# A routed-expert kernel: row gathers without empty slots, one-hot products for one pair instead of two, one more weight place, larger combination pieces, another order in the last pair

## The chip, the cores and the metric

The kernel runs on one core of a Trainium2 chip. The metric is the device time of one execution in microseconds (us). The program before was run three times: 1092.27, 1098.74 and 1100.58 us, median 1098.74. A core has five engines that work side by side: TensorE (PE; its weight loads are shown as PEld), VectorE (DVE), ScalarE (ACT), GpSimd (POOL) and SyncE (SP). They synchronise by semaphores. Sixteen DMA engines move data for all of them; each issuing engine has its own queue. Data live in SBUF (128 partitions) and in PSUM, the small memory that TensorE writes.

## What is computed

One backbone block on 512 latent tokens of width 1024 with 256 context tokens: neighbourhood attention beside a recurrent branch, merged and projected, then a mixture of experts with 32 experts, of which each token uses two, then a final RMSNorm. All is float32. The part that the change touches is the mixture:

```
def hier_moe(h, wg, bg, we, be, w1, w3, w2):
    p_top, g_idx = lax.top_k(softmax(h32 @ wg + bg), 1)      # 1 of 4 groups
    ev, e_idx = lax.top_k(le_sel, TOP_K)                     # 2 of its 8 experts
    gate = p_top * softmax(ev)
    eid = g_idx * EXPERTS_PER_GROUP + e_idx
    ...
        return (silu(xblk @ w1[e]) * (xblk @ w3[e])) @ w2[e]     # 1024 -> 512 -> 1024
    ...
    out = zeros.at[buf_tok].add(yb * buf_w[:, None])
x = x + ga2 * hier_moe(ada_rmsnorm(x, g_ffn, sh2, sc2), ...)
return rms(x) * g_final
```

## The kernel before, in words

The first part (to about 560 us) computes the modulation, the two branches and their merge. In it SP loads the weights of the up-projection (`wlo<-in_ua`, `wlo<-in_ul`, L56) and of the output projection (`woraw`, L680) in an order in which loads of expert weights (`w<-in_ew`, L908) are interleaved by hand. From about 560 to 617 us the output projection runs for 4 token tiles of 128 tokens (`outp`, matmuls L762 to L764), and behind each tile the router: logits, choice of experts, rank of the token among those of its expert (`route`). Each expert has 64 slots; two experts make a pair, and the 128 slots of a pair are the 128 rows of one gather. There are 16 pairs.

The slot table. For each token tile the kernel writes, per chosen expert, a record (token number, gate, 1/rms) into a zeroed table in DRAM, `std`, with an indirect scatter from POOL (L815, eight in all). ACT loads the eight partial tables (L885), VectorE adds them up (`stok`, L886) and casts the token numbers to integers (`toki`, L888). An empty slot holds token 0 with gate 0. `rows` (L933) is an indirect DMA from POOL that gathers, for one pair, 128 rows of the normalised stream `nd` (4 KB each) by `toki`. `turn` (L939 to L946) scales those rows by the 1/rms on ACT, transposes them on TensorE in two halves and applies the modulation while it copies them from PSUM (`xg`, the transposed input of a pair).

Pairs 0 and 1 don't wait for the table. For them `onehot0` builds a one-hot matrix (128 tokens x 256 slots) from the router's registers (L821, L822), and `gather0` (L828) multiplies the normalised tokens with it. That needs the tokens split into two parts of reduced precision, `yh` and `yl` (L803, L804). `scatter` (L961, L963) later turns the same one-hot matrices into the matrices that send results back (`ot`), and into the gates.

The mixture's loop runs over pairs `pr` and steps `k` of 128 input channels: `gu(pr, k)` (L1082) is 8 matmuls against one weight piece of 1 MB (gate and up parts of two experts). After gu(pr, 7) come silu (L976), the product `hm` (L977), its transposes (L981) and the copy `hT` (L984). Then gu(pr+1, 0), and `down(pr, v)` (L1094), two halves v of the output width with two pieces of 1 MB each. So a pair uses 12 pieces, and 192 are loaded in all. `combine` multiplies the result by the gated modulation `ga` (L992), splits it (L993, L994) and sends it back to the token tiles: for each half four pieces of two matmuls (L999, L1000), each added to `x` by VectorE (L1002). `step(c, 2)` runs two such pieces between two gu steps.

What sets the order. A scheduler keeps each engine's instructions in the order of the code, unless `queued` and `tc.issue_after` pin one behind another. Weight pieces rotate through WR + WL + 3 = 23 places of SBUF (9 on the right side, 11 on the left, 3 lent early); piece n+23 is issued by SP when the matmuls on piece n are over. Two of the first places (EARLY) are given to other buffers after their first use. `late` says which of the first loads come last in SP's order.

The last pair: the accumulators of the second half are seeded with x by matmuls with the identity (L1039), `finish` adds the last results to them (L1058), squares and sums (L1061), and scales out of PSUM (L1049, L1050). The four output tiles go out by L1051.

Of the kernel before, what the change touches and what calls it, by code (L numbers as in the profile page):

```python
# [19 lines left out]
D = 1024  # L20
# [11 lines left out]
WR, WL = 9, 11  # L32
# [5 lines left out]
def tile_block(ctx: ExitStack, tc: tile.TileContext, A, out):  # L38
# [670 lines left out]

    sg = xp.tile([128, 4, 6], F32, name="sg")  # L710
# [3 lines left out]
    for q in range(2):  # L714
        V.tensor_copy(rec[:, :, q, 0], pidx[:, 0:4])
# [13 lines left out]
    ohp = R.enter_context(pool("oh", "right"))  # L729
    oh = [ohp.tile([128, 256], F32R, name="oh", bufs=4) for _ in range(4)]  # L730
# [14 lines left out]
    l2.enter_context(pool("gap")).tile([128, 10 * 256], F32, name="gap")  # L745
    with pool("p3") as p3, ExitStack() as xtx:
# [5 lines left out]
        n2h, n2l = [], []  # L752
        def outp(nh, i):
# [107 lines left out]
        pg0 = [ps3.tile([128, 256], F32, name=z, bufs=b) for z, b in (  # L861
# [10 lines left out]
        pg0.append(ps3.tile([128, 256], F32, name="pr"))  # L872
# [5 lines left out]
    with ExitStack() as wx:  # L878
        left = [wx.enter_context(pool(f"w{i}")) for i in range(WR, WR + WL)]
        wpool += [left[4], left[10], *left[5:10], *left[0:4]]  # L880
# [5 lines left out]
        V.reduce_sum(stok.rearrange("p n k -> p (n k)"), s8[:, 0:384].rearrange("p (i x) -> p x i", i=8), axis=AX.X)  # L886
# [220 lines left out]
        for pr in range(NE // 2):  # L1107
            for k in range(1 if pr else 0, NK):
# [10 lines left out]
                if cmb and k == 1:  # L1119
                    step(cmb[0], 2)  # L1120
# [305 lines left out]
```

## Time and profile before

| | us |
|---|---|
| runs | 1092.27, 1098.74, 1100.58 (median 1098.74) |
| the profiled execution | 1095.06 |
| its span | 1093.0 |
| TensorE busy | 1019.6 (93%), granted clock 0.977 of full |
| VectorE busy | 574.7 (53%) |
| ScalarE busy | 437.3 (40%) |
| GpSimd busy | 98.4 (9%) |
| moved by DMA | 303.60 MB, mean 278 GB/s |

The span is the time between the first and last instruction in the trace. Instruction rows give start and duration, engine, line of the kernel, what is written from what, and how many; a bracket gives the idle time ahead of it and what ended it. SPq, ACTq and POOLq rows are DMA issues; their duration is that of the issue, with the time to the last issue where several stand in one row. PEclk is the clock that TensorE was granted, as a share of full speed.

### The profile page before, as it was taken

The numbers are of one execution on the slowest core, as the hardware profiler recorded it, in microseconds if no ns is written. First come the engines' busy times: TensorE is split into PE (matmuls) and PEld (weight loads), VectorE is DVE, ScalarE is ACT, GpSimd is POOL, SyncE is SP. The second block draws the span as 40 slices with busy tenths as digits, with TensorE's granted clock in tenths as the row PEclk, the third lists the DMA queues.
The fourth block names the chain that finished last, engine by engine and source line by source line (L and its number), as shares of the span: only waits on it lengthen the run. The fifth ranks groups of instructions, "written<-read, shape, count | busy, mean of one in ns | idle before, by whom it ended". The sixth has DMA issues, their size and how long they took to land. (4 is left out here: it accounts for less than half of the span.)

```text
span 1093.0 us, 13843 instructions
## 1 busy us (share of the span) xinstructions
PE 1019.6 (93%) x5148; PEld 619.8 (57%) x5148; DVE 574.7 (53%) x1172; ACT 437.3 (40%) x775; POOL 98.4 (9%) x167
## 2 busy tenths in 40 slices
PE   8998999799898989869999889999999999999995
PEld 7787768567776877657888534333333333333332
DVE  5679669567856966576547623333333353322324
ACT  4335783577387458813222222222222222222214
POOL 0012011101201120110000200000000000000001
PEclk9999999899999989989999989999999999999998
DMA  9487246425633552285694899999999999999993
GB/s 373 179 246 223 92 148 198 116 83 162 189 92 111 202 135 73 74 308 168 205 371 177 315 417 418 421 421 421 420 420 420 421 420 422 420 420 420 420 421 148
DMA packets 62857, 303.60 MB, mean 278 GB/s; under 512 B 10282, under 2 KB 10562, under 8 KB 37188
## 3 DMA queue, kind: packets, MB, share of 16 engines
q1 hardware_dynamic: 44212, 254.54, 58.7%
q0 software_dynamic: 12512, 40.93, 12.1%
q10 hardware_dynamic: 6064, 7.22, 1.9%
q8 instruction: 41, 0.67, 0.2%
q14 instruction: 28, 0.23, 0.1%
HBM read 286.72 MB, written 9.65 MB: 271 GB/s over the span
## 5 line engine op out<-in xcount | busy, mean ns | idle before, releaser
L1082 PE MATMUL g<-w,xg 128*64 128x512 f32 x1024 | 240.5, 605 | 2.6 <-DMA w<-in_ew 2.4
L1082 PEld LDWEIGHTS g<-w,xg 128*64 128x64 f32 x1024 | 66.2, 137 | 129.9 <-issue 114.6
L48 PE MATMUL pj<-hh,whi 128*128 128x512 f32 x320 | 132.1, 413 | 2.4 <-ACT gi L498 1.9
L49 PE MATMUL pj<-hl,whi 128*128 128x512 f32 x320 | 128.2, 400 | 0.0
L50 PE MATMUL pj<-hh,wlo 128*128 128x512 f32 x320 | 127.9, 400 | 0.0
L1094 PE MATMUL y<-w,hT 128*64 128x512 f32 x512 | 114.1, 594 | 4.8 <-DMA w<-in_ew 4.8
L1002 DVE TENSOR_TENSOR x<-x,pc 128x512 f32<-128x512 f32 x121 | 77.8, 684 | 70.5 <-PE pc L1000 70.5
L946 ACT ACTIVATE xg<-pg,sh2col,s2col 128x128 f32<-128x128 f32 x112 | 42.1, 457 | 131.5 <-PE pg L943 131.5
L60 DVE TENSOR_TENSOR wlo<-wlo,whi 128x1024 fp32r<-128x1024 f32 (+1 forms) x60 | 68.9, 1148 | 46.8 <-ACT whi L59 46.7
L59 ACT CAST whi<-wlo 128x1024 fp32r<-128x1024 f32 (+1 forms) x60 | 59.4, 990 | 82.1 <-DMA wlo<-in_wcol 44.3
L993 ACT CAST y_h<-hm 128x512 fp32r<-128x512 f32 x31 | 19.2, 619 | 161.0 <-PE pc L999 93.7
L1094 PEld LDWEIGHTS y<-w,hT 128*64 128x64 f32 x512 | 35.1, 137 | 81.9 <-issue 60.1
L992 DVE TENSOR_TENSOR hm<-y,ga 128x512 f32<-128x512 f32 x31 | 21.4, 692 | 110.6 <-PE y L1094 102.2
L48 PEld LDWEIGHTS pj<-hh,whi 128*128 128x128 f32 x320 | 61.4, 192 | 19.9 <-ACT gi L498 3.5
L50 PEld LDWEIGHTS pj<-hh,wlo 128*128 128x128 f32 x320 | 61.1, 191 | 15.1
L49 PEld LDWEIGHTS pj<-hl,whi 128*128 128x128 f32 x320 | 61.5, 192 | 12.4
L977 DVE SCALAR_TENSOR_TENSOR hm<-hm,stok,g 128x512 f32<-128x512 f32 x14 | 10.5, 748 | 95.2 <-PE g L1082 95.2
L999 PE MATMUL pc<-y_h,ot 128*128 128x512 f32 x121 | 54.4, 449 | 1.2 <-ACT y_h L993 1.2
L999 PEld LDWEIGHTS pc<-y_h,ot 128*128 128x128 f32 x121 | 22.8, 188 | 53.3 <-issue 48.7
L1000 PE MATMUL pc<-y_l,ot 128*128 128x512 f32 x121 | 48.5, 400 | 0.1
L496 PE MATMUL pj<-xc,ga 128*128 128x256 f32 (+1 forms) x128 | 47.7, 500 | 0.0
L933 POOL DMA_INDIRECT xr<-nd,toki x14 | 13.2, 944 | 367.0 <-PE pt L981 287.7
(393 smaller groups left out, 1753.9 us busy)
## 6 DMA issues: line engine op xcount, KB each, us to landing
w<-in_ew SPq DMA_DIRECT2D x191, 1024.0 KB
wlo<-in_wcol SPq DMA_DIRECT2D x40, 512.0 KB
m<-in_wm POOLq DMA_DIRECT2D x32, 512.0 KB, 3.9
wm<-in_wm SPq DMA_DIRECT2D x8, 1024.0 KB
bias<-in_rpb POOLq DMA_DIRECT2D x32, 128.0 KB, 2.4
kr<-khl POOLq DMA_DIRECT2D x16, 256.0 KB, 6.4
gd<-ga ACTq DMA_DIRECT2D x16, 256.0 KB
wlo<-in_ul SPq DMA_DIRECT2D x8, 512.0 KB
```

Of the source, the lines that this page charges most:

```text
L48: PE.matmul(o, wh, hh, start=start, stop=False)
L49: PE.matmul(o, wh, hl, start=False, stop=False)
L50: return PE.matmul(o, wl, hh, start=False, stop=stop)
L59: S.copy(hi[:, :n], raw[:, :n])
L60: V.tensor_tensor(lo[:, :n], raw[:, :n], hi[:, :n].bitcast(F32), op=ALU.subtract)
L496: m = PE.matmul(pg[:, 0:n], lw[:, 128 * w:128 * w + 128], xc[:, s0:s0 + n], start=True, stop=True)
L946: S.activation(xg[:, k, :], pg[:, k % 4, :], AF.Identity, bias=sh2col[:, k:k + 1], scale=s2col[:, k:k + 1])
L999: PE.matmul(pc, ot[:, i, :], y_h, start=True, stop=False)
L1000: m = PE.matmul(pc, ot[:, i, :], y_l, start=False, stop=True)
L1002: V.tensor_add(x2[:, i, ns], x2[:, i, ns], pc)
L1082: m = PE.matmul(pgu[pr][v][64 * e:64 * e + 64, :], xg[pr][:, k, 64 * e:64 * e + 64], w[:, v, e, :], start=(k == 0), stop=(k == NK - 1))
L1094: m = PE.matmul(py[64 * e:64 * e + 64, :], hT[:, k, 64 * e:64 * e + 64], w[:, k % 2, e, :], start=(k == 0), stop=(k == 3))
```

## The change

Nine edits. (1) WL is 12 instead of 11: one more place of 1 MB, and SP's order begins with three expert pieces where it began with two. `late` moves by three with it, and the places are handed out in another order. (2) The one-hot matrices have 128 columns (pair 0 only) and carry 1/rms as their value, so that `gather0` multiplies `x2` itself in one matmul where there were two, and `yh` and `yl` are gone. (3) The table's token numbers are stored plus one; after the sum one is subtracted, and an empty slot becomes a number past the last token. (4) The gather has a bound, past which a row is left out; its target is one tile `xr`, zeroed once. (5) Pairs 1 to 15 are gathered, pair 1 in the place where pair 2's gather was issued. (6) All pairs take gate and return matrix from the table. (7) `combine` runs four pieces at once, after gu(pr+1, 0) with down(pr), and after gu(pr+1, 3), where it ran two pieces at four places; transposes, pieces and broadcasts share four PSUM banks. (8) In the last pair three seeds run after gu(15, 4), and the first half's pieces lie inside the second half's down. (9) Some small operations of the final norm are taken out of its loop.

```
-WR, WL = 9, 11
+WR, WL = 9, 12
...
-        V.tensor_copy(rec[:, :, q, 0], pidx[:, 0:4])
+        V.tensor_scalar(rec[:, :, q, 0], pidx[:, 0:4], 1.0, None, op0=ALU.add)
...
-                S.activation(n2h[i][:, hs], x2[:, i, hs], AF.Copy, scale=st[:, 4:5])
-                V.scalar_tensor_tensor(n2l[i][:, hs], x2[:, i, hs], st[:, 4:5], n2h[i][:, hs].bitcast(F32),
-                                       op0=ALU.mult, op1=ALU.subtract)
...
-            V.tensor_scalar(t, iot[:, 0:256], sgt[i][:, 0:1], None, op0=ALU.is_equal)
-            V.scalar_tensor_tensor(oh[i], iot[:, 0:256], sgt[i][:, 1:2], t, op0=ALU.is_equal, op1=ALU.add)
+            V.tensor_scalar(oh[i], iot[:, 0:128], sgt[i][:, 0:1], r, op0=ALU.is_equal, op1=ALU.mult)
+            V.tensor_scalar(t, iot[:, 0:128], sgt[i][:, 1:2], r, op0=ALU.is_equal, op1=ALU.mult)
+            V.tensor_tensor(oh[i], oh[i], t, op=ALU.add)
...
-                for h in (n2h, n2l):
-                    PE.matmul(pg0[k], h[i][:, 128 * k:128 * k + 128], oh[i],
-                              start=(i == 0 and h is n2h), stop=(i == 3 and h is n2l))
+                PE.matmul(pg0[k], x2[:, i, 128 * k:128 * k + 128], oh[i], start=(i == 0), stop=(i == 3))
...
-        toki = p4.tile([128, NE // 2], I32, name="toki")
-        V.tensor_copy(toki, stok[:, :, 0])
...
+        V.tensor_scalar(stok[:, :, 0], stok[:, :, 0], 1.0, None, op0=ALU.subtract)
+        V.tensor_scalar(tokx, stok[:, :, 0], 0.0, 2.0 * T, op0=ALU.is_lt, op1=ALU.mult)
+        V.tensor_tensor(toki, tokx, stok[:, :, 0], op=ALU.add)
+        xr = p4.tile([128, D], F32, name="xr")
+        G.memset(xr, 0.0)
...
-        late = (*range(WR + 5, WR + 9), EARLY[1], *range(WR + 9, WR + WL + 3))
+        late = (*range(WR + 8, WR + 12), EARLY[1], *range(WR + 12, WR + WL + 3))
...
-            G.indirect_dma_start(xr, None, nd[:, :], bass.IndirectOffsetOnAxis(ap=tok, axis=0))
+            G.indirect_dma_start(xr, None, nd[:, :], bass.IndirectOffsetOnAxis(ap=tok, axis=0), bounds_check=T - 1,
+                                 oob_is_err=False)
...
-        cmb, xr = [], rows(toki[:, 2:3])
+        rows(toki[:, 1:2])
+        cmb = []
...
-                if cmb and k == 1:
-                    step(cmb[0], 2)
                 if cmb and k == 3:
-                    step(cmb[1], 2)
+                    step(cmb[1], 4)
...
-                if 0 < pr < LAST and k == 5:
-                    xg[pr + 1] = p4.tile([128, NK, 128], F32, name="xg", bufs=2)
-                    turn(xr, xg[pr + 1], 0, stok[:, pr + 1, 2:3])
-            if cmb:
-                step(cmb[1], 2)
+                if pr < LAST and k == 5:
+                    xg[pr + 1] = halves()
+                    turn(xg[pr + 1], 0, stok[:, pr + 1, 2:3])
+                if pr == LAST and k == 4:
...
+                    for i in range(3):
+                        with queued():
+                            m = seed(i)
...
-            if pr > 1:
-                ot = places(stok[:, pr, 0:1])
+            ot = places(stok[:, pr, 0:1])
...
-                step(cmb[0], 2)
+                step(cmb[0], 4)
...
+            py = down(pr, 1, range(0, 3))
+            for i in range(3):
+                norm_half(next(part))
+            py = down(pr, 1, range(3, 4), py)
             norm_half(next(part))
-            with tc.issue_after(m):
-                py = down(pr, 1)
```

Three places show what stands where. First TensorE in the first pair, before (L1082 is gu, L961 and L963 turn the one-hot matrices, L981 transposes hm, L1094 is down):

```order
L1082 MATMUL g_5657<-w,xg 64x512 x2
L1082 MATMUL g_5658<-w,xg 64x512 x2
L961 MATMUL pt<-ident,oh 128x128 x4
L963 MATMUL pg<-sg,oh 128x6 x4
L1082 MATMUL g_5657<-w,xg 64x512 x2
L1082 MATMUL g_5658<-w,xg 64x512 x2
L981 MATMUL pt<-ident,hm 128x128 x4
L1082 MATMUL g_5733<-w,xg 64x512 x2
L1082 MATMUL g_5734<-w,xg 64x512 x2
L1094 MATMUL y_5739<-w,hT 64x512 x8
```

The same place of the change (L1079 is gu, L945 transposes gathered rows `xr`, L1032 spreads the modulation `ga`):

```order
L1079 MATMUL g_5604<-w,xg_5540 64x512 x2
L1079 MATMUL g_5605<-w,xg_5540 64x512 x2
L945 MATMUL pc<-ident,xr 128x128 x4
L1079 MATMUL g_5604<-w,xg_5540 64x512 x2
L1079 MATMUL g_5605<-w,xg_5540 64x512 x2
L1079 MATMUL g_5604<-w,xg_5540 64x512 x2
L1079 MATMUL g_5605<-w,xg_5540 64x512 x2
L1032 MATMUL pc<-ga_5654,ones 128x512 x2
L945 MATMUL pc<-ident,xr 128x128 x4
L981 MATMUL pc<-ident,hm 128x128 x4
L1079 MATMUL g_5690<-w,xg_5630 64x512 x2
L1079 MATMUL g_5691<-w,xg_5630 64x512 x2
```

The two gu steps ahead of hm's transposes, 6 and 7, now stand behind transposes of gathered rows, the first half of pair 1's.

Second ACT at the same time, before (L885 loads the table, L976 is silu, L939 scales gathered rows):

```order
L885 DMA s_5575<-std_85 128x48
L885 DMA s_5575<-std_86 128x48
L966 CAST ot<-pt 128x512
L976 ACT_TABLE_LOAD
L976 ACTIVATE hm<-g_5657 128x512
L984 COPY hT<-pt 128x512
L1034 COPY ga_5695<-pc 128x512 x2
L993 CAST y_h<-hm 128x512
L939 ACTIVATE xr<-xr,stok 128x1024
```

And now (L878 loads the table, L941 scales, L948 copies the transposed rows):

```order
L878 DMA s_5523<-std_85 128x48
L878 DMA s_5523<-std_86 128x48
L941 ACTIVATE xr<-xr,stok 128x1024
L948 ACTIVATE xg_5630<-pc,sh2col,s2col 128x128 x4
L976 ACT_TABLE_LOAD
L976 ACTIVATE hm<-g_5604 128x512
L1033 COPY ga_5654<-pc 128x512 x2
L948 ACTIVATE xg_5631<-pc,sh2col,s2col 128x128 x4
L984 COPY hT<-pt 128x512
```

The scaling of the gathered rows moved from behind the first pair's silu, copies and cast to directly behind the table's loads.

Third TensorE at the end, before (L1039 seeds, L1094 down, L999 and L1000 the pieces, L1058 the last products):

```order
L1039 MATMUL g_8048<-x_4626,ident 128x512
L1094 MATMUL y_8051<-w,hT 64x512 x8
L1094 MATMUL y_8076<-w,hT 64x512 x8
L999 MATMUL pc<-y_h,ot 128x512
L999 MATMUL pt<-y_h,ot 128x512
L999 MATMUL y_8121<-y_h,ot 128x512
L1000 MATMUL pc<-y_l,ot 128x512
L1000 MATMUL pt<-y_l,ot 128x512
L1000 MATMUL y_8121<-y_l,ot 128x512
L1058 MATMUL pg<-hm,ot 128x512
```

And now (L1038 seeds, L1092 down, L998 and L999 the pieces, L1057 the last products):

```order
L1038 MATMUL g_8017<-x_4626,ident 128x512
L1092 MATMUL y_8019<-w,hT 64x512 x8
L1092 MATMUL y_8033<-w,hT 64x512 x6
L998 MATMUL pc<-y_h,ot 128x512
L999 MATMUL pc<-y_l,ot 128x512
L998 MATMUL g_8032<-y_h,ot 128x512
L999 MATMUL g_8032<-y_l,ot 128x512
L998 MATMUL y_8019<-y_h,ot 128x512
L999 MATMUL y_8019<-y_l,ot 128x512
L1092 MATMUL y_8033<-w,hT 64x512 x2
L998 MATMUL pc<-y_h,ot 128x512
L999 MATMUL pc<-y_l,ot 128x512
```

One seed stands ahead of down(15) where four stood, and three of the pieces moved from behind it to ahead of its last two weight blocks.

## Rows read from the trace of the kernel before

**Rows 1.** Windows: PE, PEld, DVE, ACT, POOL busy (instructions), clock, DMA share, GB/s.
```profile
600.00:620.00 20.00, 15.25 (x136) 12.63 (x136) 18.41 (x114) 7.65 (x21) 7.44 (x8) 1.00 0.74 282
615.00:620.00 5.00, 4.92 (x35) 3.35 (x35) 3.62 (x15) 2.90 (x8) 2.46 (x3) 1.00 0.21 41
620.00:630.00 10.00, 10.00 (x48) 3.16 (x44) 0.00 (x0) 0.00 (x0) 0.00 (x0) 1.00 1.01 411
930.00:1050.00 120.00, 113.45 (x500) 40.87 (x500) 35.32 (x56) 26.64 (x54) 2.82 (x3) 1.00 1.01 421
1070.00:1080.00 10.00, 10.00 (x42) 4.11 (x39) 4.39 (x9) 2.36 (x7) 0.93 (x1) 1.00 0.08 33
```
**Rows 2.** Waits of SP's queue in 930 to 1093: total, times, longest.
```profile
SPq L908 <- DMA w<-in_ew: 99.5, 46, 2.7
```
**Rows 3.** Timeline of ACT: silu of pairs 2 and 10, start and duration.
```profile
696.43 0.60 ACT L976 ACTIVATE hm<-g 128x512 f32<-128x512 f32 x1 [1.23 <-PE g L1082]
...
915.38 0.60 ACT L976 ACTIVATE hm<-g 128x512 f32<-128x512 f32 x1 [1.23 <-PE g L1082]
```
**Rows 4.** Timeline of SP: issues of expert weights before 621.
```profile
476.30 0.80 SPq L908 DMA_DIRECT2D w<-in_ew  x2
...
534.61 13.61 SPq L908 DMA_DIRECT2D w<-in_ew  x8
...
564.63 38.00 SPq L908 DMA_DIRECT2D w<-in_ew  x9
...
617.69 3.12 SPq L908 DMA_DIRECT2D w<-in_ew  x5
```
**Rows 5.** Timeline of TensorE from 617, and the window 637 to 640.
```profile
617.85 12.24 PE L1082 MATMUL g<-w,xg 128*64 128x512 f32 x56
...
636.03 0.66 PE L981 MATMUL pt<-ident,hm 128*128 128x128 f32 x4 [2.69 <-DVE hm L977]
636.61 3.53 PE L1082 MATMUL g<-w,xg 128*64 128x512 f32 x8
...
637.00:640.00 3.00, 3.00 (x10) 0.81 (x8) 0.44 (x1) 0.30 (x1) 0.00 (x0) 0.50 1.01 409
```
**Rows 6.** Timeline: the slot table's way on ACT's queue, DVE, POOL and ACT.
```profile
623.53 9.13 ACTq L885 DMA_DIRECT2D s<-std  x3
...
639.56 0.80 DVE L886 TENSOR_REDUCE stok<-s 128x48 f32<-128x384 f32 x1 [3.60 <-DMA s<-std]
640.40 0.17 DVE L888 CAST toki<-stok 128x16 int32<-128x16 f32 x1
...
641.56 1.00 POOL L933 DMA_INDIRECT xr<-nd,toki  x1 [22.74 <-issue]
...
651.25 1.15 ACT L939 ACTIVATE xr<-xr,stok 128x1024 f32<-128x1024 f32 x1 [1.09 <-DMA xr<-nd,toki]
```
**Rows 7.** Groups of VectorE in 595 to 617: busy, mean ns.
```profile
L822 DVE SCALAR_TENSOR_TENSOR oh<-iot,sg,oht 128x256 fp32r<-128x256 f32 x4 | 1.9, 481 | 0.0
```
**Rows 8.** DMA issues: KB each, median us to landing; the gathers' own spread.
```profile
bias<-in_rpb POOLq DMA_DIRECT2D x32, 128.0 KB, 2.4
...
std<-rec,si POOLq DMA_INDIRECT x8, 6.2
...
DMA to landing us min/median/max: 8.4/9.7/9.9
```
**Rows 9.** Timeline of TensorE behind the early expert pieces.
```profile
489.57 0.50 PE L48 MATMUL pj<-oh,whi 128*128 128x512 f32 x1 [2.83 <-ACT whi L59]
```
**Rows 10.** Timeline of TensorE in the last pair.
```profile
1062.40 1.94 PE L1082 MATMUL g<-w,xg 128*64 128x512 f32 x8 [0.55 <-DMA w<-in_ew]
...
1069.29 7.09 PE L1094 MATMUL y<-w,hT 128*64 128x512 f32 x32
1076.30 0.50 PE L999 MATMUL pc<-y_h,ot 128*128 128x512 f32 x1
...
1077.80 1.02 PE L1058 MATMUL pg<-hm,ot 128*128 128x512 f32 x2
```

More of the change, by code (lines that the diff above doesn't have):

```diff
@@ L751, in tile_block @@
         lgs = p3.tile([128, 4, 36], F32, name="lgs")
-        n2h, n2l = [], []
+        oh = [p3.tile([128, 128], F32, name=f"oh{i}") for i in range(4)]
         def outp(nh, i):
@@ L955, in scatter @@
         def scatter(oh, x):
-            pt = ps4.tile([128, 4, 128], F32, name="pt")
-            pq = ps4.tile([128, 256], F32, name="pg")
-            with queued():
-                for i in range(4):
-                    PE.transpose(pt[:, i, :], oh[i].bitcast(F32), ident)
-                for i in range(4):
-                    m = PE.matmul(pq[:, 0:6], oh[i].bitcast(F32), sg[:, i, :], start=(i == 0), stop=(i == 3))
-            tail[0] = tail[0] and m.ins
+            pt = ps4.tile([128, 4, 128], F32, name="pc", bufs=4)
+            pq = ps4.tile([128, 256], F32, name="pc", bufs=4)
+            for i in range(4):
+                PE.transpose(pt[:, i, :], oh[i].bitcast(F32), ident)
+            for i in range(4):
+                PE.matmul(pq[:, 0:6], oh[i].bitcast(F32), sg[:, i, :], start=(i == 0), stop=(i == 3))
             ot = p5.tile([128, 4, 128], F32R, name="ot", bufs=2)
@@ L983, in act, with combine @@
             hT = p5.tile([128, 4, 128], F32, name="hT")
-            return hT, S.copy(hT, pt).ins
-        def combine(v, py, ot, last=False):
+            return hT, S.copy(hT, pt).ins, pt
+        def combine(v, py, ot, banks=None):
             ns = slice(512 * v, 512 * v + 512)
@@ L995, in combine @@
             for i in range(4):
-                pc = ps4.tile([128, 512], F32, name=("y0" if i == 2 else "pt")) if last and i else ps4.tile(
-                    [128, 512], F32, name="pc", bufs=2)
+                pc = banks[i] if banks else ps4.tile([128, 512], F32, name="pc", bufs=4)
                 with queued():
@@ L1038, in seed, with finish @@
         def seed(i):
[L1039 to L1041 removed]
+            return PE.matmul(acc[i], ident, x2[:, i, 512:1024], start=True, stop=False)
+        def finish(py, ot):
             ns = slice(512, 1024)
@@ L1081, in gu, with down @@
                     for e in range(2):
-                        m = PE.matmul(pgu[pr][v][64 * e:64 * e + 64, :], xg[pr][:, k, 64 * e:64 * e + 64],
+                        m = PE.matmul(pgu[pr][v][64 * e:64 * e + 64, :], xg[pr][k // 4][:, k % 4, 64 * e:64 * e + 64],
                                       w[:, v, e, :], start=(k == 0), stop=(k == NK - 1))
             tail[0] = m.ins
-        def down(pr, v):
-            py = ps4.tile([128, 512], F32, name=f"y{v}")
-            for k in range(4):
+        def down(pr, v, ks=range(4), py=None):
+            py = py or ps4.tile([128, 512], F32, name=f"y{v}")
+            for k in ks:
                 if k % 2 == 0:
-                    w = weights(pr, 8 + 2 * v + k // 2)
+                    dw[0] = weights(pr, 8 + 2 * v + k // 2)
+                w = dw[0]
                 with queued():
@@ L1213, in tile_block @@
                 for v in range(2):
-                    PE.matmul(pgu[v], xg[:, k, 0:128], w[:, v, :], start=(k == 0), stop=(k == NK - 1))
-            hT, after = act(pgu, gate)
+                    PE.matmul(pgu[v], xg[k // 4][:, k % 4, :], w[:, v, :], start=(k == 0), stop=(k == NK - 1))
+            hT, _, _ = act(pgu, gate)
             for v in range(2):
```

107 lines of the change are left out of this document (46 added, 61 removed).

## The prediction

> **What bounds the kernel now.** I read the windows first. From 620 on the DMA engines are full: 411 GB/s at a share of 1.01 over 620–630, 421 GB/s over 930–1050, and almost nothing after 1071 (1070–1080: share 0.08, that is 0.8 us of transfers) [rows 1]. What they move are the experts' weights, 192 pieces of 1.0486 MB, 12 for each of the 16 pairs of experts. At 421 GB/s a piece takes 1.0486 / 0.421 = 2.49 us. Second, the waits of SP at the end: in 930–1093 its weight loads wait 99.5 us for earlier loads, and for almost nothing else [rows 2]. TensorE is the nearer limit earlier: its silu starts of pair 2 and pair 10 lie 218.95 us apart, 27.37 a pair [rows 3], while 12 pieces and one gather take 31.1. So the stream sets the end, and the kernel ends a fixed tail after its last piece. A change is worth what it does to (a) the moment from which the stream never stops, and what has landed then, (b) the bytes after it, (c) the tail.
>
> For (a): SP had issued 2 pieces at 476, 8 from 534.61, and nine from 564.63 to 602.63, 19 in all, when the next five went out at 617.69 [rows 4]. In between the DMA engines ran dry: share 0.21 in 615–620 [rows 1]. So 19 pieces lay in SBUF at about 619.8, two microseconds behind that issue.
>
> Last, the start of the MoE on TensorE: gu(0,·), 8 steps of 8 matmuls, runs from 617.85 to 633.34 with only the one-hot transposes between; after 2.69 us of waiting the granted clock is 0.50 in 637–640, that is the lower level, 1.2 GHz, and a step takes 3.53 instead of some 1.75 us (12.24 / 7) [rows 5]. The pair's last step ends at 633.34, where that wait begins. Beside it, and hidden, runs the round trip of the slot table: its last three loads wait on ACT's queue until 632.66 (they reuse semaphores of weight pieces still in flight), VectorE gets the table at 639.56, POOL issues the gather at 641.56, and ACT scales its rows at 651.25 [rows 6]. Nobody waits for that: these rows are pair 2's, and pairs 0 and 1 came out of the one-hot products.
>
> **The change, part by part.** *One-hot products for pair 0 only.* Pair 1 is now gathered, and TensorE's order puts the transposes of its rows between gu(0,5) and gu(0,6). So the hidden round trip becomes a wait of TensorE. It starts near 617.85 + 6 x 1.75 = 628, or 2 to 3 us sooner, as VectorE loses the yl products and half of each one-hot matrix; the sum doesn't hang on the start. It ends so:
> - The seventh and eighth table loads now wait for pieces 26 and 27. Piece 15 waits on an out-projection matmul near 599.7, so data flow from 601.7 (the same two microseconds), with 14 landed. Before, 600–620 carried 282 GB/s x 20 us = 5.6 MB, of which I put 0.8 (an estimate) to other transfers than pieces 15 to 19. Full, at 421 GB/s, 601.7–619.8 carries 7.6; less 0.8 that is 6.5 pieces, so 20.5 have landed at 619.8 (1.5 more than before). At 411 GB/s (2.55 a piece) piece 27 lands at 636.4 and piece 29 at 641.5.
> - The last load: 6.9 us before (632.66 to 639.56) with the stream full behind it. Lower bound 2.4, the median landing of the bias loads [rows 8]. Only two pieces are queued with it now; I take 5.5: 642.2.
> - VectorE: 0.80, three small steps like toki's 0.17, and two places products, which I set at 0.48 each from the old one-hot row [rows 6, 7]: 2.3, giving 644.5; POOL's issue one more, 645.5.
> - The gather: 9.7 us to landing as before, with 128 rows beside a full stream; lower bound 6.2, the small scatters [rows 8]. 69 rows beside an idle stream: I take 7.5. Then ACT's 1.15: 654.2.
>
> TensorE thus stands for 26 to 29 us. After that it runs four transposes (0.6), gu(0,6) at the low clock (3.5) and gu(0,7) (2 to 2.7), to 661; then silu and hm, and gu(1,0) ends near 665.5.
>
> Does the stream suffer? There are now 24 places: pieces 25 to 29 go into those that gu(0,0) to gu(0,5) free (two of these were lent out and are gone), 30 needs gu(0,7) and 31 needs gu(1,0). So after piece 29 at 641.5 the DMA engines stand, but for 30, until 665.5 + 2 = 667.5; 30 pieces have landed then and 162 remain. **This is the main term.**
>
> *Row gathers leave out empty slots.* Counted from the inputs' routing, 1,024 of the 2,048 slots are filled, 71 in pair 0, 69 in pair 1, so pairs 2 to 15 gather 884 rows of 4 KB, 3.62 MB or 8.6 us of stream. Before, 14 gathers moved all 128 slots: 14 x 1.25 = 17.4 us.
>
> Sum for the stream: 667.5 + 162 x 2.49 (403.4) + 8.6 = 1079.5. The same sum for before, 619.8 + 173 x 2.49 (430.8) + 17.4 = 1068.0, is 3 short of 1071 (table loads, broadcast rows, a slower start); half of that still lies ahead at 667.5. So the last piece lands at 1081, **10 later**.
>
> *One more weight place* lets a third piece go at 476.7. It stands in front of the up-projection weights that SP issues next, whose cast TensorE already awaited 2.83 us before 489.57 [rows 9]. A piece is 2.49 us; delay 0 to 2.5, I take **+1**, since the load's wait on an earlier piece may absorb part.
>
> *Larger combination pieces.* Two switches between gu and pieces fewer a pair. Even if that saves nothing, TensorE at 27.37 a pair ends gu(15,7) at 661 + 15 x 27.37 = 1072; the stream, 10 later than before, lets it end at 1074 (before: 1064.34 [rows 10]). So it is worth 0, hidden behind the stream, with 2 us to spare and whatever it does save. On the other side, four PSUM banks now serve transposes and pieces, and a fifth piece has to wait until VectorE has added an earlier one. I bound that by 1 us a pair, about two wide VectorE operations like the 0.48-us one [rows 7]; then it shows.
>
> *Last pair.* Down(15) began at 1069.28, 4.9 us after gu(15,7), behind four seeds; its weights were there at 1071, so it could have been up to 2.8 earlier before its last piece held it [rows 1, 10]. Three seeds now run at k = 4. The three combination pieces between its end and the final matmuls (1076.30 to 1077.80) move inside it and cost the same there. Between 0 and -2.8; I take **-2**, since the last results still pass one after the other through squares and scaling.
>
> Sum: 1095.06 (the profiled run: span 1093.0 and 2.1 around it) + 10 + 1 - 2 = **1104**. That run lies 3.7 under the median of those shown, 1098.74; against it 1104 is +0.5%. A change of about 1% (11 us) is what a measurement of this kernel can tell.
>
> **The rivals.** *A short stall* (0.20). By the lower bounds, load 2.4 and gather 6.2, TensorE resumes 4.4 earlier: 1100. The Trainium skill, "DMA: Bandwidth & Descriptors", section "Anatomy of one DMA — SWDGE (gpsimd) path", fits a transfer as about 2.0 us plus bytes over 436 GB/s. An estimate by it: 2.1 us for the 24 KB load and 2.7 for the 0.28 MB gather, 8.2 less than I took, so 1096. The trace speaks against it beside a full stream (6.9 and 9.7); no run here shows an idle one.
>
> *No hole at all: faster* (0.08). If the table lands before the stream runs out of places, nothing stops: the last piece would land 1.5 x 2.49 + 8.8 = 12.5 earlier than before, with the shorter tail 1081. It decides at the resumption of TensorE: each microsecond before 654 is one off the sum, so for -11 against before it has to resume by about 635. Against it: piece 27 alone lands after 636, and scaling, gather and table lie behind it.
>
> *The gathers cost as much as before* (0.09): if a skipped slot still costs its transfer's time, +8.8: 1113.
>
> *TensorE takes over* (0.10): if the pc banks cost 1 us a pair, 28.4 a pair puts gu(15,7) at 1087 where the stream allows 1074, 13 more: 1117 at most.
>
> **How the numbers follow.** My forecast has 0.53, on 1100 to 1112. The range 1094 to 1117 holds it with the short stall, dear gathers and the cheaper part of TensorE's case, and leaves out the hole-free case. Faster by over 1% needs under 1088: 0.08. Slower needs over 1110 against the median: gathers 0.09, TensorE 0.10, the upper edge of the forecast with a dear third piece 0.13, together 0.32. Within 1%: 0.60.
>
> **What would show it.** Right: TensorE idle from about 626 to 650–657 with the transposes of pair 1 behind it; a granted clock of about 0.5 right after; GB/s near nothing in 645–660; SP's weight issues missing there; gathers past 667 at about half their bytes; down(15) starting within 3 us of gu(15,7); SP still waiting for loads, not for matmuls, at the end. Wrong: no window near 0 GB/s after 640, or TensorE resuming before 640 (then faster), or waits of TensorE on banks and of SP on matmuls in 930–1050 (then the stream no longer bounds).

## The result, and the profile after

The changed kernel takes 1107.95 us (median; 1105.9 to 1113.24) where the kernel before takes 1098.47 in the same series: 1.0102 of before, 95% interval 1.0077 to 1.0127. A second series gave 1.0088 (1.0057 to 1.0119). So it is slower, by about 10 us. (A ratio compares the means of runs of one series, so it isn't the quotient of the two medians.) Its profiled run took 1111.29, above its median, and the profiled run of before 1095.06, below its own. 3.3 us of that difference arise before 476, where both programs run the same instructions. I therefore compare traces from the first matmul of the output projection (545.5 before, 549.9 after; it stands there in the traces, not near 560 as the description of the kernel has it) to the end of the span: **547.5 before, 559.4 after, +11.9**; the second profile of the changed kernel gives 559.4 as well.

First the windows of the changed kernel (columns as in [rows 1]):

```profile
600.00:620.00 20.00, 16.04 (x145) 14.41 (x143) 16.88 (x126) 3.23 (x13) 7.36 (x8) 1.00 0.77 306
620.00:640.00 20.00, 10.52 (x48) 3.36 (x48) 0.96 (x3) 1.15 (x4) 1.53 (x2) 0.83 1.02 419
640.00:645.00 5.00, 0.00 (x0) 0.00 (x0) 0.00 (x0) 0.00 (x0) 0.00 (x0) 0.50 0.99 387
645.00:650.00 5.00, 0.00 (x0) 0.00 (x0) 2.02 (x6) 0.00 (x0) 0.00 (x0) 0.50 0.05 13
650.00:660.00 10.00, 3.89 (x12) 1.71 (x14) 0.00 (x0) 3.81 (x6) 1.06 (x1) 0.50 0.10 28
660.00:665.00 5.00, 5.00 (x20) 1.75 (x19) 0.75 (x1) 1.86 (x4) 0.00 (x0) 0.94 0.28 75
665.00:670.00 5.00, 5.00 (x27) 1.75 (x26) 0.00 (x0) 2.03 (x6) 1.02 (x1) 1.00 0.77 274
930.00:1050.00 120.00, 118.50 (x542) 45.90 (x540) 38.34 (x62) 27.73 (x58) 3.97 (x4) 1.00 1.01 421
```

Where [rows 1] showed a full stream from 620 on, there is now a hole: 13 GB/s in 645–650, 28 in 650–660, 75 in 660–665. (The 28 are the gather of pair 1 itself: 69 rows of 4 KB in 10 us.) TensorE does nothing in 640–650, at the lower clock of 1.2 GHz (0.50).

The stream also ends in another way than before. Windows of the kernel before, then of the changed kernel:

```profile
1066.00:1068.00 2.00, 2.00 (x9) 1.10 (x8) 0.40 (x1) 1.17 (x2) 0.00 (x0) 1.00 1.02 418
1068.00:1070.00 2.00, 2.00 (x8) 0.63 (x8) 0.00 (x0) 0.91 (x2) 0.00 (x0) 1.00 0.74 301
1070.00:1072.00 2.00, 2.00 (x12) 0.66 (x10) 0.00 (x0) 0.00 (x0) 0.00 (x0) 1.00 0.41 166
```

```profile
1078.00:1080.00 2.00, 2.00 (x12) 0.72 (x10) 0.00 (x0) 0.00 (x0) 0.00 (x0) 1.00 0.87 363
1080.00:1082.00 2.00, 2.00 (x12) 0.57 (x8) 0.00 (x0) 0.29 (x1) 0.00 (x0) 1.00 0.79 324
1082.00:1084.00 2.00, 1.08 (x9) 0.56 (x6) 0.75 (x1) 0.30 (x1) 0.00 (x0) 1.00 0.60 246
1084.00:1086.00 2.00, 2.00 (x9) 0.61 (x10) 0.00 (x0) 1.85 (x2) 0.00 (x0) 1.00 0.23 92
```

Before, the DMA engines went from full to empty within some 4 us; now they thin out over some 10. In the trace a weight load ends with 16 signals, as many as there are DMA engines, and TensorE starts on a piece behind the last of them (in pair 14 at 1037.37, the signals ran from 1026.30 to 1037.32). For the last load these signals come from 1068.56 to 1072.29 before, and from 1076.09 to 1087.04 in the changed kernel. So the last weights are there at 1087, and some of the engines are done 11 us earlier than others. Where that comes from is seen at x10.

TensorE's timeline in the first pair, which answers to [rows 5]:

```profile
620.15 10.52 PE L1079 MATMUL g<-w,xg 128*64 128x512 f32 x48 [0.60 <-ACT xg L899]
656.11 1.11 PE L945 MATMUL pc<-ident,xr 128*128 128x128 f32 x4 [25.44 <-ACT xr L941]
657.16 5.36 PE L1079 MATMUL g<-w,xg 128*64 128x512 f32 x16
```

Six gu steps, then 25.44 us of waiting for the scaled rows of pair 1, then the two last steps, at the lower clock up to about 660. What they waited for, the slot table's way (timeline of ACT's queue, DVE, POOL, ACT; then the gathers' landing times), which answers to [rows 6, 8]:

```profile
634.21 7.96 ACTq L878 DMA_DIRECT2D s<-std  x6
...
647.67 0.80 DVE L879 TENSOR_REDUCE stok<-s 128x48 f32<-128x384 f32 x1 [26.71 <-DMA s<-std]
...
649.59 0.17 DVE L885 TENSOR_TENSOR toki<-s,stok 128x16 int32<-128x16 f32 x1
...
650.67 1.06 POOL L935 DMA_INDIRECT xr<-nd,toki  x1 [29.13 <-issue]
...
654.91 1.15 ACT L941 ACTIVATE xr<-xr,stok 128x1024 f32<-128x1024 f32 x1 [33.77 <-DMA xr<-nd,toki]
...
DMA to landing us min/median/max: 4.1/8.2/8.7
```

The eighth load goes out at 642.17: it waits for the semaphore of weight piece 27, which lands at 641.76, and uses the same one for itself. It takes 5.5 us. The sums take 2.1, and the gather beside an empty stream 4.1. SP's weight issues, but for one at 662.56, are missing until 667.35.

The other half of the story is at the end. TensorE's waits from 680 on (total, times, longest):

```profile
PE pc L981 <- DVE hm L977: 5.6, 15, 0.9
PEld g L1079 <- DMA w<-in_ew: 5.0, 13, 0.8
PEld y L1092 <- DMA w<-in_ew: 2.5, 7, 0.8
```

Its matmuls no longer wait for weights; before, they did at the end ([rows 10] shows one such wait). Only weight loads of TensorE (PEld) wait, up to 0.8 us, while matmuls still run. The margin is small all the same: between the last piece of down(13) and gu(14,7) three weight pieces land 0.04 us ahead of the first matmul on them. Its silu starts on ACT (pairs 0, 1, 14 and 15; [rows 3] of before), and its last pair:

```profile
661.70 0.60 ACT L976 ACTIVATE hm<-g 128x512 f32<-128x512 f32 x1 [1.57 <-PE g L1079]
...
690.58 0.60 ACT L976 ACTIVATE hm<-g 128x512 f32<-128x512 f32 x1 [1.23 <-PE g L1079]
...
1048.44 0.60 ACT L976 ACTIVATE hm<-g 128x512 f32<-128x512 f32 x1 [1.37 <-PE g L1079]
...
1081.71 0.60 ACT L976 ACTIVATE hm<-g 128x512 f32<-128x512 f32 x1 [16.02 <-PE g L1079]
...
1055.69 7.48 PE L1092 MATMUL y<-w,hT 128*64 128x512 f32 x32
...
1074.38 2.84 PE L1038 MATMUL pc<-x,ident 128*128 128x512 f32 x6
...
1084.88 6.23 PE L1092 MATMUL y<-w,hT 128*64 128x512 f32 x28
...
1092.63 1.08 PE L1092 MATMUL y<-w,hT 128*64 128x512 f32 x4
...
1094.50 2.84 PE L1057 MATMUL pc<-hm,ot 128*128 128x512 f32 x6
```

Thirteen pairs take 357.86 / 13 = 27.53 us each; the last takes 33.27, with the three seeds (2.84), the spread of the final gain (1.98) and a stretch at the lower clock in it. The last weights, there at 1087.04, are used at 1092.63.

### The profile page after: what moved, and what is told of

Same layout as the page of the kernel before. It is cut to its first block, busy times and chain, and to the rows that moved or that the text cites. A ratio compares the mean times of both kernels' runs of the same rounds, so it can differ in the third digit from the quotient of the medians.

```text
span 1109.3 us, 13809 instructions
## 1 busy us (share of the span) xinstructions
PE 1016.6 (92%) x5132; PEld 624.7 (56%) x5132; DVE 569.3 (51%) x1156; ACT 434.5 (39%) x770; POOL 101.2 (9%) x169
## 3 DMA queue, kind: packets, MB, share of 16 engines
q0 software_dynamic: 12656, 37.50, 11.1%
## 5 line engine op out<-in xcount | busy, mean ns | idle before, releaser
L1079 PE MATMUL g<-w,xg 128*64 128x512 f32 x1024 | 236.9, 605 | 0.6 <-ACT xg L899 0.6
L1079 PEld LDWEIGHTS g<-w,xg 128*64 128x64 f32 x1024 | 68.3, 137 | 130.5 <-issue 123.6
L1092 PE MATMUL y<-w,hT 128*64 128x512 f32 x512 | 113.5, 595 | 0.0
L948 ACT ACTIVATE xg<-pc,sh2col,s2col 128x128 f32<-128x128 f32 x120 | 45.2, 457 | 155.3 <-PE pc L945 155.2
L1092 PEld LDWEIGHTS y<-w,hT 128*64 128x64 f32 x512 | 36.6, 138 | 74.4 <-issue 66.7
L977 DVE SCALAR_TENSOR_TENSOR hm<-hm,stok,g 128x512 f32<-128x512 f32 x16 | 11.9, 747 | 105.4 <-PE g L1079 105.4
L998 PE MATMUL pc<-y_h,ot 128*128 128x512 f32 x122 | 51.4, 422 | 0.0
L999 PE MATMUL pc<-y_l,ot 128*128 128x512 f32 x122 | 48.0, 394 | 0.0
L48 PE MATMUL pj<-oh,whi 128*128 128x512 f32 x96 | 39.5, 415 | 7.4 <-ACT whi L59 4.8
```

Source lines behind the costliest of these rows:

```text
L48: PE.matmul(o, wh, hh, start=start, stop=False)
L948: S.activation(xg[z][:, k % 4, :], pg[:, k % 4, :], AF.Identity, bias=sh2col[:, k:k + 1], scale=s2col[:, k:k + 1])
L998: PE.matmul(pc, ot[:, i, :], y_h, start=True, stop=False)
L999: m = PE.matmul(pc, ot[:, i, :], y_l, start=False, stop=True)
L1079: m = PE.matmul(pgu[pr][v][64 * e:64 * e + 64, :], xg[pr][k // 4][:, k % 4, 64 * e:64 * e + 64], w[:, v, e, :], start=(k == 0), stop=(k == ...
L1092: m = PE.matmul(py[64 * e:64 * e + 64, :], hT[:, k, 64 * e:64 * e + 64], w[:, k % 2, e, :], start=(k == 0), stop=(k == 3))
```

## The experiments

Beside the median and the ratio to the kernel before in the same series, I give two stretches of the profile that the early spread doesn't touch: A, from the first matmul of the output projection to the end of the span, and B, from down(14) to the end. The kernel before had medians of 1097.3 to 1098.5 in the five series, so medians of different series compare to about 1 us, ratios better.

| kernel | median us | ratio (95%) | A | B |
|---|---|---|---|---|
| before | 1098.47 | 1 | 547.5 | 52.8 |
| changed | 1107.95 | 1.0102 (1.0077–1.0127) | 559.4 | 53.6 |
| x17 changed, again | 1106.65 | 1.0088 (1.0057–1.0119) | 559.4 | 53.6 |
| x1 table on POOL | 1098.02 | 0.9994 (0.9973–1.0016) | 548.7 | 53.3 |
| x8 transposes later | 1103.47 | 1.0057 (1.0034–1.0079) | 553.6 | 53.5 |
| x3 skip only | 1091.22 | 0.9925 (0.9902–0.9949) | 542.1 | 52.7 |
| x2 one-hot for two | 1090.95 | 0.9952 (0.9925–0.9980) | 546.0 | 53.6 |
| x10 full gathers | 1114.01 | 1.0153 (1.0100–1.0207) | 566.0 | 53.9 |
| x6 gain by its load | 1109.50 | 1.0111 (1.0083–1.0139) | 559.7 | 55.5 |
| x9 pieces cover hm | 1108.81 | 1.0098 (1.0069–1.0127) | 559.0 | 53.2 |
| x12 two of these on x2 | 1093.41 | 0.9957 (0.9934–0.9980) | 544.0 | 55.4 |
| x7 seeds late | 1108.00 | 1.0092 (1.0067–1.0118) | 558.0 | 52.3 |
| x13 no seeds | 1107.12 | 1.0091 (1.0066–1.0115) | 556.1 | 50.3 |
| x14 third piece later | 1108.73 | 1.0118 (1.0087–1.0148) | 558.4 | 53.6 |
| x15 three edits | 1102.65 | 1.0050 (1.0027–1.0074) | 550.2 | 53.6 |
| x16 and the row later | 1101.41 | 1.0039 (1.0014–1.0064) | 547.6 | 53.4 |

**Is it the wait for the table?**

> The changed kernel, with one edit: the eight loads of the slot table go out on POOL's queue instead of ACT's, so that they no longer wait for weight pieces 25 to 27. Theory A (the wait for pair 1's rows opens a hole of some 20 us in the weight stream and puts TensorE back by 25 us): the last scatter goes out near 619.6 and takes 6, the load 5, the sums 2, the gather 8 beside a full stream, so TensorE resumes near 643 instead of 656, and the kernel takes 1107.95 - 12 = 1096. Theory B (the loss lies in the early third weight piece ahead of the up-projection): no change, 1108. Theory C (TensorE's loop has become slower by the larger combination pieces and the other order): the resumption moves but the loop's period stays at 27.5, so also some 1096, with TensorE still without a wait for weights at the end.

```
-            S.dma_start(s8[:, 48 * i:48 * i + 48], by_slot[i])
+            G.dma_start(s8[:, 48 * i:48 * i + 48], by_slot[i])
```

Measured 1098.0: one line of the changed kernel brings back the loss. Its trace (the last sum, POOL's issue of the gather, TensorE's wait):

```profile
629.14 0.17 DVE L885 TENSOR_TENSOR toki<-s,stok 128x16 int32<-128x16 f32 x1
...
630.21 1.07 POOL L935 DMA_INDIRECT xr<-nd,toki  x1 [8.03 <-DMA w<-in_ew]
...
640.01 1.11 PE L945 MATMUL pc<-ident,xr 128*128 128x128 f32 x4 [14.45 <-ACT xr L941]
```

The wait falls from 25.44 to 14.45 us, A from 559.4 to 548.7. (The bracket of the gather names a weight load; what came last ahead of it is the sum at 629.14.) Theory A holds in place and size (11 less wait, 10.7 less time); theory B is out as the main cause. The wait isn't gone: 14.45 us of it are left, and kernels without it take 1091 (x3, x2).

> The changed kernel, with one edit: the first half of pair 1's transposes stands behind gu(0,7) in the first pair, no longer between gu(0,5) and gu(0,6). Theory A: the gather lands at the same time (about 655), but two gu steps (5.4 us at the low clock) and the places of two pieces come ahead of the wait: the hole shrinks by one piece or two, TensorE is 4 to 5 us ahead afterwards, and the kernel takes 1103. Theories B and C: 1108.

```
-                if pr < LAST and k == 5:
+                if pr < LAST and k == (5 if pr else 7):
```

Measured 1103.47, A 5.8 less: as expected. (1.4 of the 5.8 are no part of the edit: its trace lacks the stretch at the lower clock in the last pair, of which the last section tells.) The wait behind gu(0,5) costs two slow gu steps and the places of the pieces that these free.

**What the parts bring without the wait.**

> The kernel before with one edit: the gathers leave out empty slots (token numbers plus one in the table, a bound on the gather, one zeroed target). Theory A with a stream that bounds: 884 rows instead of 1792, 8.8 us less of stream, 1098.5 - 8.8 = 1089.7. Rival: a skipped slot costs the transfer's time all the same: 1098.5. Second rival: the stream was not the bound at the end, and TensorE takes over: between the two, no less than 1095.

```
-            G.indirect_dma_start(xr, None, nd[:, :], bass.IndirectOffsetOnAxis(ap=tok, axis=0))
+            G.indirect_dma_start(xr0, None, nd[:, :], bass.IndirectOffsetOnAxis(ap=tok, axis=0), bounds_check=T - 1,
+                                 oob_is_err=False)
```

(with the table's numbers plus one, and one zeroed target; only the gather is shown). Measured 1091.2, 0.9925: faster than both kernels. The software queue moves fewer bytes; the page's row before, and that of x3:

```profile
q0 software_dynamic: 12512, 40.93, 12.1%
```

```profile
q0 software_dynamic: 12512, 37.22, 11.3%
```

3.71 MB less, which is the 908 empty slots of pairs 2 to 15 at 4 KB, in as many packets. The gain is 6.8 by the medians of its series, 8.2 by the ratio and 5.4 in A, of the 8.8 that the bytes are worth. In the trace the last weights land 5.3 earlier than before, counted from the output projection, and the 16 signals of the last load lie 10.9 us apart, before 3.7.

> The kernel before with two groups of the edits: gathers without empty slots, and the larger combination pieces with the other order in the last pair. One-hot products still serve pairs 0 and 1, with 23 weight places. Theory A: no wait in the first pair, so no hole; the stream ends 8.8 earlier than before (13.5 gathers at half the bytes) and the tail is 2 shorter: 1098.5 - 10.8 = 1087.7. Theory B: the third early piece is gone, so the loss of 9.5 is gone: 1098 or below. Theory C (the loop's edits are what costs): 1103 to 1108, with a period of 27.5 and a last pair of 33 us.

```
-WR, WL = 9, 12
+WR, WL = 9, 11
...
-        rows(toki[:, 1:2])
+        rows(toki[:, 2:3])
...
+                if pr < 2 and k == (2 if pr else EARLY[1] + 1):
+                    ot, gate, _ = scatter([z[:, 128 * pr:128 * pr + 128] for z in oh], pidx[:, pr:pr + 1])
```

(Of the change it keeps the gathers that leave slots out, the combination in fours and the last pair's order; it has neither the one-hot product for pair 0 alone nor the twelfth weight place.) Measured 1090.95, 3 above theory A. Without the wait the loss is gone, so A's cause holds. But against x3 the larger pieces and the last pair's new order bring nothing: the same median, and A is 3.9 longer. (In this kernel four pieces stand at once behind the spread of the modulation row, which adds a wait of 1.19 and a stretch at the lower clock, 0.50 in 648 to 652: the first period is 36.5 us, in x3 33.2.)

**Which limit binds the changed kernel?**

> The changed kernel, with one edit: an empty slot reads row 0 again, so that the gathers move all 128 rows (8.8 us more of stream past pair 1). Theory S: 1108 + 8.8 = 1117. Theory P: the last weights land near 1083 in the changed kernel's trace and are used at 1092.6, so 9 us of stream are free: 1108 to 1110, with TensorE waiting for weights in the last pairs only.

```
-        V.tensor_scalar(tokx, stok[:, :, 0], 0.0, 2.0 * T, op0=ALU.is_lt, op1=ALU.mult)
+        V.tensor_scalar(tokx, stok[:, :, 0], 0.0, 1.0, op0=ALU.is_lt, op1=ALU.mult)
```

Measured 1114.0, A 6.6 longer: between the two theories. TensorE's waits from 930 on:

```profile
PE y L1092 <- DMA w<-in_ew: 4.6, 5, 1.5
PE pc L981 <- DVE hm L977: 2.6, 6, 0.9
```

The windows at its end:

```profile
1082.00:1084.00 2.00, 2.00 (x12) 0.43 (x6) 0.00 (x0) 0.60 (x1) 0.00 (x0) 1.00 1.00 410
1084.00:1086.00 2.00, 1.08 (x7) 0.69 (x6) 0.75 (x1) 0.23 (x1) 0.00 (x0) 1.00 0.65 262
1086.00:1088.00 2.00, 2.00 (x10) 0.62 (x10) 0.00 (x0) 1.85 (x3) 0.00 (x0) 1.00 0.33 133
```

With all rows moved, the stream ends within some 4 us again, and the 16 signals of the last load lie 4.4 us apart, in the changed kernel 11.0. Only the empty slots differ. So leaving them out relieves some DMA engines more than others: in the changed kernel the spread is 1.8 us near the first pair and grows with the gathers. A piece is there when the last engine has delivered, and the last weights land only 6.5 us later in x10 (543.7 from the output projection against 537.2). That is what A shows, 6.6. Theory S holds, with 8.8 too high a price; theory P started from a misreading, as the last weights land at 1087.04, 5.6 us ahead of their use, and the stream has nothing to spare in pairs 13 and 14. Which engines get fewer rows, no view shows.

> The changed kernel, with one edit: the final gain is spread over the partitions by its load and no longer by two one-row matmuls of TensorE (1.98 us) in the last pair but one. Theory P (TensorE bounds the changed kernel from its resumption to the end, the stream has slack): 1.98 less, and if the low granted clock that follows those matmuls in the trace (0.64 in 1052 to 1056) is theirs, some 1.7 more: 1107.95 - 3.7 = 1104.3. Theory S (the stream still bounds): 1108.

```
-                    broadcast(gfin, A["gfin"])
+                    SP.dma_start(gfin, A["gfin"].to_broadcast([128, D]))
```

Measured 1109.5, no gain. TensorE in down(14) of x6:

```profile
1051.01 1.94 PE L1092 MATMUL y<-w,hT 128*64 128x512 f32 x8 [0.55 <-DMA w<-in_ew]
1053.40 1.94 PE L1092 MATMUL y<-w,hT 128*64 128x512 f32 x8 [0.45 <-DMA w<-in_ew]
1055.89 1.94 PE L1092 MATMUL y<-w,hT 128*64 128x512 f32 x8 [0.55 <-DMA w<-in_ew]
1058.37 1.94 PE L1092 MATMUL y<-w,hT 128*64 128x512 f32 x8 [0.54 <-DMA w<-in_ew]
```

TensorE is there earlier and then runs at the stream's beat, one piece each 2.48 us. Down(14) ends 513.5 after the start of the output projection, in the changed kernel 513.3. Both limits meet there.

> The changed kernel, with one edit: the second four combination pieces of a pair stand behind gu(pr,7), ahead of hm's transposes, instead of behind gu(pr,3). They then cover TensorE's wait for hm, 0.33 us and more in each of 14 pairs. Theory P: the period falls from 27.47 to 27.1, 14 x 0.35 = 5 less: 1103. Theory S: 1108.

```
-                if cmb and k == 3:
+                if cmb and k == 3 and pr == LAST:
                     step(cmb[1], 4)
...
+            if cmb and pr < LAST:
+                step(cmb[1], 4)
             if pr < LAST:
                 turn(xg[pr + 1], 1, None)
```

Measured 1108.8, A 0.4 less. The waits for hm are gone except one of 0.9; TensorE has 3.7 us of waits for weights instead. The period falls more than expected, to 26.6, but one pair takes 35.5: there the edit opened a new wait.

```profile
PE pc L945 <- ACT xr L941: 5.5, 1, 5.5
```

This stall took most of the saving. It isn't what keeps the time, though: behind it the weights land 0.04 us ahead of their use in pairs 13 and 14, and the last ones at 536.9 from the output projection, as in the changed kernel (537.2). Theory P alone falls with x6, x9 and x10; so does S alone, with the next two.

> The changed kernel without the three seed matmul pairs behind gu(15,4): 2.84 us of TensorE are left out, and with them the residual of the second half of three token tiles. Theory L (TensorE bounds from down(14) to the end): 1108 - 2.8 = 1105. Theory S (the last weights bound): 1108.

```
-                PE.matmul(acc[i], ot[:, i, :].bitcast(F32), yv, start=False, stop=True)
+                PE.matmul(acc[i], ot[:, i, :].bitcast(F32), yv, start=(i < 3), stop=True)
...
-                    for i in range(3):
-                        with queued():
-                            m = seed(i)
-                        tail[0] = m.ins
```

The median is only 0.8 lower (1.0091, whose interval takes in both answers). In the trace B falls from 53.6 to 50.3, by a little more than the 2.84 us of the seeds. So behind down(14) TensorE binds, not the last weights.

> The changed kernel, with one edit: the three seeds of the last pair stand behind gu(15,7), as before the change, and no longer behind gu(15,4). The prediction's step (seeds ahead of the last weights bring up to 2.8 us, because the weights come last): 1108 + 2.8 = 1110.8. Theory L (in the last pair TensorE, not the weights, bounds): the same matmuls in another place, less the 0.92 us of waiting for hm that they now cover: 1107.

```
-                if pr == LAST and k == 4:
+                if pr == LAST and k == 7:
```

Measured 1108.0; B is 1.3 less. The prediction's step would have shown 2.8 more. Theory L holds.

> The kernel with one-hot products for two pairs, gathers without empty slots and larger pieces (1090.95), with two edits more: the second four pieces behind gu(pr,7), and the final gain spread by its load. There TensorE's and the stream's ends lie close: TensorE's last pair ends at 1060 and the last weights land near 1063, to be used near 1070. Theory P: 14 x 0.35 + 3.7 = 8.6 less TensorE, of which 7 to 8 show before the last weights stop it: 1083. Theory S: 1091.

```
-                if cmb and k == 3:
+                if cmb and k == 3 and pr == LAST:
...
+            if cmb and pr < LAST:
+                step(cmb[1], 4)
...
-                    broadcast(gfin, A["gfin"])
+                    SP.dma_start(gfin, A["gfin"].to_broadcast([128, D]))
```

(These are the edits of x9 and x6, made on x2.) Measured 1093.4 (0.9957, as x2's 0.9952): A falls by 2.0, and B grows to 55.4, as TensorE waits for weights in down(14) and gu(15,·). One pair takes 33.9 us here, with the same stall as in x9, so TensorE did not save the 8.6 either. Theory P falls for x2 as well.

**The third early piece, and all together.**

> The changed kernel, with one edit: the third early weight piece goes out behind the last early load of the output projection (near 512) and no longer at 476. Theory: TensorE's wait for the up-projection's weights near 490 falls from 4.7 to 5.4 us (four traces of kernels with three early pieces) to the 2.8 to 3.9 of those with two; 1.5 to 2 less, 1106.2. Rival: the wait moves to the next load behind the piece, 1108.

```
...
-            with tc.issue_after(loaded[0]) if n in late[4:] else nullcontext():
+            with tc.issue_after(loaded[0]) if n in late[4:] else tc.issue_after(anchor) if n == 13 else nullcontext():
```

Measured 1108.7, no gain: the rival. TensorE's wait near 490 falls to 3.2 us, but two later waits for weights of the up-projection bring the sum to 4.8 again. From SP's first early piece to the output projection, traces with two early pieces take 68.0 to 69.5 us (before, x2, x3, x12), those with three 70.0 to 70.9 (changed, x1, x6 to x10, x13, x17), and this one 71.9. So the third piece costs 1 to 2, and later on it costs more.

> The changed kernel with three edits together: table loads on POOL's queue (1098.0 alone), pair 1's first transposes behind gu(0,7) (4.5 less alone), third early piece later. If the three work on different parts of the loss (the table's wait, what stands behind it, the up-projection): 1098.0 - 4.5 - 1.7 = 1091.8, below both kernels. If the first two cure the same loss: 1096 to 1098.

```
-            S.dma_start(s8[:, 48 * i:48 * i + 48], by_slot[i])
+            G.dma_start(s8[:, 48 * i:48 * i + 48], by_slot[i])
...
-                if pr < LAST and k == 5:
+                if pr < LAST and k == (5 if pr else 7):
```

(These are the edits of x1 and x8, made on x14.) Measured 1102.65, worse than x1 alone; the expectation fell. Its trace shows a new wait in the place of the old one. The row of the modulation, loaded behind the weights, arrives 12.66 us late, and its matmuls stand ahead of pair 1's transposes:

```profile
645.76 3.78 PE L1032 MATMUL pc<-ga,ones 1*128 1x512 f32 x4 [12.66 <-DMA ga<-modd]
```

> The kernel x15_all, with one edit: the two matmuls that spread the modulation row over the partitions stand behind down(0), as in the kernel before, and no longer ahead of pair 1's transposes, where TensorE waited 12.7 us for the row's load. Theory W (that wait took the place of the one removed): the gather issued near 636 lands near 644, TensorE resumes 5 to 6 us earlier than in x15_all and gu(1,0) follows at once; 1102.65 - 6 to - 9 = 1094 to 1097. Rival (moving the third early piece, which made TensorE's way from 476 to the output projection 2 to 3 us longer, is what cost): 1102.

```
...
-                    broadcast(ga2, modd[3:4, :])
+                    broadcast(ga2, modg)
...
+                if pr == 0:
+                    with queued():
+                        broadcast(ga2, None)
```

Measured 1101.4, 5 above theory W; in the trace A is 2.6 less, of which 1.7 is a last pair without the stretch at the lower clock. TensorE waits as long as before, now for the gathered rows themselves:

```profile
647.95 1.97 PE L945 MATMUL pc<-ident,xr 128*128 128x128 f32 x8 [12.67 <-ACT xr L941]
```

So that wait did not hold x15 up by its own size: the rows come 3.3 us later than in x1, counted from the output projection. By A, x16 (547.6) is 1.1 better than x1, but 1.7 of that is the last pair's clock again, which fell in x1's trace. By the medians it is 3.4 worse. The loss lies ahead of A: from SP's first early piece to the output projection x16's trace takes 75.4 us, x15's 73.3 and x1's 70.3. The rival, the later third piece, fits that, but the same edit took 71.9 in x14. Why this stretch differs so, and why the rows come later than in x1, I can't show; that stays open.

> The changed kernel as it is, again. If the sum of the prediction (+9 us against a run of the kernel before of the same series) is right: 1.0082 of before. If the loss is what the first ratio says: 1.0102.

1.0088: both answers lie in its interval.

## Why the prediction was right or wrong

**Right: the mechanism, its place and its chain.** I said that TensorE stops behind gu(0,5) for pair 1's rows. It did, for 25.44 us (forecast 26 to 29). I said that the eighth load waits for piece 27 and takes 5.5 us (5.5), the sums 2.3 (2.1), and that the gather takes 7.5 (4.1, below my lower bound of 6.2); and that 0.5 is the clock behind it (0.50), and that the stream stands but for one piece until 667.5, two microseconds behind SP's issue. It stood from about 645, and SP's issue came at 667.35, in a trace that runs 4.4 us late from the output projection on: 2.6 earlier than forecast, as the gather was faster. x1 and x8 show by their size that this wait is the loss.

**Right in number, partly by luck: the stream 10 later.** Counted from the output projection the last weights land 10.3 later (526.8 before, 537.2 after). But the hole was 2.6 shorter than I had it, and the left-out rows brought some 2 less than their bytes.

**Right in part: the empty slots.** x3 gives 5.4 of 8.8 in A without the hole, x10 6.6 within it. I priced the rows by the mean of the DMA engines; a weight piece waits for the last of them. The rival "the gathers cost as much as before" is out.

**Wrong: the last pair's term.** I took -2 for it, arguing that the last weights bind there and the seeds stood in their way. B says +0.8. In the changed kernel the last weights land 5.6 us before their use. TensorE binds behind down(14); the seeds cost there what they cost in any place (x7, x13), and the last period is 33.27 us where I had 27.37.

**Wrong for the same reason: "worth 0, hidden behind the stream, with 2 us to spare".** I compared both limits at gu(15,7) and gave TensorE 15 equal periods, 410.6 us. From the first silu to the last it took 420.0; 5.9 of the 9.4 that were missing lie in the last period. The other periods stayed where they were, 27.47 in most pairs against 27.31: two switches are saved, but 0.33 us of waiting for hm stand open, which two pieces seem to have covered before. The two limits meet earlier, in pairs 13 and 14 (x6, x9, x10); from there TensorE has 33 us of last pair. So the rival "TensorE takes over" came in for the last pair, without the waits on banks that I gave it.

**Wrong: the step from the sum to the forecast.** The stretch ahead of the output projection was forecast at +1 (measured about +1), the rest at +8 (measured +11.9 in A: +11.1 up to down(14), with some 1.4 of lower clock behind the spread of the final gain in it, and +0.8 behind it). +9 in all would have been 1107.5 on the median of 1098.47. I put it on the profiled run instead, 3.4 under that, and read 1104 as +0.5% and within 1%. I also took 1% for what a measurement can tell; the interval of the ratio is a quarter of that to either side. A sum made against a low run has to be carried over as a difference.

**The fit for the gather.** The fit of the Trainium skill, "DMA: Bandwidth & Descriptors", section "Anatomy of one DMA — SWDGE (gpsimd) path" (some 2.0 us plus bytes over 436 GB/s), gave 2.7 us for the gather and 2.1 for the load beside an idle stream. The page gives it for DMAs issued from GpSimd; the gather is one, the table's loads on ACT's queue are not. Here the gather took 4.1 with nothing else moving, the load 5.5 with two pieces still under way. The measurement decides: the fit is short by 1.4 for the gather, and nearer than the 7.5 that I took.

## What to carry to other kernels

When a change takes a shortcut for the first step of a pipeline away, follow the hidden chain that it exposes to its first wait on an unrelated semaphore: here the loads of a small table waited for weight pieces because they reused the semaphores of those pieces, and another queue for these loads was worth 10.7 of the 11.9 us. When a stall eats the slack of an engine that was hidden, compare the two limits at every stage up to the end, not at the end alone, and with the last, untypical stage at its own price. Price bytes that are left out by what the most loaded DMA engine saves, not by their sum. Carry a sum from a profile over as a difference, not as a time, when the profiled run is not the median.

## What the runs showed of the hardware that I had not expected

A gather that leaves rows out has as many packets as one that doesn't (12512 in both) and 3.71 MB less; its median time to landing falls only from 9.7 to 8.8 us in x3, and with the stream idle it was 4.1. And the rows that stay are spread unevenly over the DMA engines: the 16 signals of one weight load lie 11 us apart at the end (x3, changed kernel), with all rows moved 3.7 to 4.4 (before, x10).

The granted clock can fall with TensorE busy. Behind the one-row matmuls that spread the final gain (from 1050.76 on), the changed kernel ran at the lower level, 1.2 GHz, for a while; without them, in x6, the clock stayed full though TensorE waited for weights there. Windows of the changed kernel, then of x6:

```profile
1050.00:1052.00 2.00, 1.83 (x7) 1.08 (x8) 0.12 (x1) 1.95 (x6) 0.00 (x0) 1.00 1.03 430
1052.00:1054.00 2.00, 2.00 (x8) 0.44 (x8) 0.00 (x0) 1.09 (x2) 0.00 (x0) 0.79 1.00 418
1054.00:1056.00 2.00, 2.00 (x8) 0.70 (x6) 0.00 (x0) 0.00 (x0) 0.00 (x0) 0.50 1.01 422
```

```profile
1050.00:1054.00 4.00, 2.99 (x15) 0.89 (x14) 0.00 (x0) 0.00 (x0) 0.00 (x0) 1.00 1.02 426
```

It isn't so each time. In eleven traces these matmuls stand directly behind hm's transposes and a wait of 0.33 us. In seven of them (changed, x1, x7, x10, x13, x15, x17) the clock fell, and gu(15,0) took 3.05 to 3.57 us; in four (x2, x8, x14, x16) it took 1.94. With the seeds in the same place, the last period is 33.2 to 33.3 us where it fell and 31.6 to 31.9 where it didn't. In the kernel before the same matmuls at 1038.31, with a gu step ahead of them, left the clock at 1.00. What decides it these runs don't show.
